# Row means of a 32 x 512 x 1024 array: rows laid out by partition, sums on two engines, and a last tile loaded in shrinking pieces

## The chip, the core and the metric

The kernel runs on one core of a Trainium2 chip. The metric is device time in microseconds (us); a smaller number is better. Three runs of the kernel before gave 173.33, 173.07 and 173.38 us, a median of 173.33.

Names used below: VectorE (DVE in the profile) and ScalarE (ACT) are the two engines that can sum along a row here. SyncE's queue (SP, SPq) issues the transfers between the chip's main memory and the on-chip memory, and 16 DMA engines carry them out. The on-chip memory has 128 partitions; a tile is a piece of it, written as partitions x elements per partition. A landing is the moment at which a transfer's completion is seen.

## The reference

```python
batch, seq, dim = 32, 512, 1024          # x: float32, divisor: 1024.0

def reference(x, divisor):
    return (np.sum(x, axis=-1) / divisor).astype(np.float32)
```

The input is 32 x 512 = 16384 rows of 1024 float32 numbers, 4 KB each, 67.1 MB in all. The output is one number per row, 64 KB. Each input number is read once and added once, so there is nothing to use again.

## The kernel before

The rows are cut into 16 tiles of 1024 rows (`ntiles`, line 25). Within a tile, partition p holds 8 rows that follow each other in memory (`R = 8`), that is 8192 numbers or 32 KB; partition p + 1 holds the next 32 KB. One tile is thus a contiguous block of 4 MB in main memory.

The loop in line 33 does two things per tile: SyncE issues one load of the tile (line 35), and VectorE sums each of the 8 rows (line 36, one instruction with 8 results per partition) into `res`, a tile of 128 x 16 x 8 that stays on the chip. After the loop one instruction on VectorE multiplies all of `res` by 1/divisor (line 37), and one transfer stores it (line 38). Since `res` holds the 8 results of each tile side by side, while in main memory the 8 results of a tile's partition lie apart from those of the next tile, the store writes 128 x 16 runs of 8 numbers, 32 B each.

The order of the work is set by the program's order on each engine and by buffers. The pool `sb` has three buffers for the tile `t`: the loads of the first three tiles are issued at once, and each later load waits in SyncE's queue until VectorE has summed the tile three back. Loads are carried out in the order of their issue, so a load that is issued while another is under way stands behind it. The three operations of the program touch one another only through these waits: reduction on load, load on reduction three back, scaling on all reductions, store on scaling. ScalarE does nothing.

Of the kernel before, what the change touches and what calls it, by code (L numbers as in the profile page):

```python
# [1 line left out]

# [4 lines left out]


@with_exitstack
def kernel(  # L10
    ctx: ExitStack,
    tc: tile.TileContext,
    x: bass.AP,
    divisor: float,
    out: bass.AP,
):
    nc = tc.nc
    xf = x.flatten_outer_dims()
    N, D = xf.shape
    P = nc.NUM_PARTITIONS  # L20
    scale = 1.0 / float(divisor)

    R = 8
    rows_per_tile = P * R
    ntiles = N // rows_per_tile
    assert ntiles * rows_per_tile == N

    xr = x.tensor.reshape((ntiles, P, R, D)).ap()
    out_v = out.tensor.reshape((ntiles, P, R)).ap().rearrange("t p r -> p t r")

    with tc.tile_pool(name="sb", bufs=3) as pool, tc.tile_pool(name="res", bufs=1) as rpool:
        res = rpool.tile([P, ntiles, R], mybir.dt.float32)
        for i in range(ntiles):
            t = pool.tile([P, R, D], mybir.dt.float32)
            nc.sync.dma_start(out=t, in_=xr[i])
            nc.vector.reduce_sum(out=res[:, i, :], in_=t, axis=mybir.AxisListType.X)  # L36
        nc.vector.tensor_scalar_mul(out=res, in0=res, scalar1=scale)  # L37
        nc.sync.dma_start(out=out_v, in_=res)


# [1 line left out]
_INS = ['x', 'divisor']  # L42
_OUTS = [((32, 512), 'float32')]
#: Inputs that are plain numbers.
_NUMBERS = {'divisor': 1024.0}


def kernel(**inputs):
    import numpy as _np
    import concourse.bacc as _bacc  # L50
    import concourse.tile as _tile
    from concourse import mybir as _mybir
    from concourse.bass_utils import run_bass_kernel_spmd as _run

    nc = _bacc.Bacc("TRN2", target_bir_lowering=False, num_devices=1)  # L55
    arrays, args = {}, []
    for name in _INS:
        if name in _NUMBERS:
            args.append(_NUMBERS[name])
            continue  # L60
        a = _np.ascontiguousarray(inputs[name])
        if a.dtype.kind in "iu":
            a = a.astype(_np.int64)
        arrays[f"in_{name}_dram"] = a
        args.append(nc.dram_tensor(f"in_{name}_dram", a.shape, _mybir.dt.from_np(a.dtype), kind="ExternalInput").ap())
    for i, (shape, dtype) in enumerate(_OUTS):
        dt = _mybir.dt.from_np(_np.dtype(dtype))
        args.append(nc.dram_tensor(f"out_{i}_dram", shape, dt, kind="ExternalOutput").ap())
    with _tile.TileContext(nc) as tc:
        kernel(tc, *args)  # L70
    r = _run(nc, [arrays], core_ids=[0])
    got = tuple(r.results[0][f"out_{i}_dram"] for i in range(len(_OUTS)))
    return got[0]
```

## Time and profile before

| | |
|---|---|
| median of three runs | 173.33 us (173.07 to 173.38) |
| span of the profiled execution, first to last instruction (its own time; nothing around it is recorded) | 171.5 us |
| VectorE busy | 139.2 us (81%), 17 instructions |
| one reduction of a tile (line 36) | 8686 ns, 16 times |
| VectorE idle before reductions, all waiting for a load | 28.5 us, of which 13.1 for the first |
| scaling (line 37) | 226 ns |
| loads: 16 of 4096 KB | 20.4 us from issue to landing (median) |
| store: one of 64 KB | 3.0 us from issue to landing |
| main memory traffic | 67.11 MB read, 0.07 MB written, 392 GB/s over the span |

How to read it: the span is the time of one profiled execution on the core; the medians of the runs include what lies around it as well. In the rows of busy digits, the span is cut into 40 slices, and each digit is the busy share of a slice in tenths. A transfer's time from issue to landing includes the time in which it stands behind earlier ones, so the 20.4 us of a load are more than its own share of the DMA engines' time. In the timeline, the bracket behind an instruction is the idle time of its engine before it and what ended that. A row with "x3" stands for three instructions.

### The profile page before, as it was taken

What the parts mean: (1) busy time and instruction counts of PE and PEld (TensorE: products, weight loads), DVE (VectorE), ACT (ScalarE), POOL (GpSimd) and SP (SyncE); (2) the same over time, 40 slices, a digit from 0 to 9 for tenths busy, and PEclk for the clock granted to TensorE, in tenths of its full rate; (3) what the DMA queues carried; (4) which work ended last, traced back from release to release, by engine and by line L of the source; (5) the groups of instructions that cost most, each with busy time, mean ns of one, the idle gap of its engine ahead of it and who ended that gap; (6) DMA issues with size and microseconds to landing.
All of it is one profiled execution on the core that took longest, in us unless ns stands there. A gap on an engine that the chain in (4) does not pass through costs nothing.

```text
span 171.5 us, 92 instructions
## 1 busy us (share of the span) xinstructions
DVE 139.2 (81%) x17; POOL 0.2 (0%) x4
## 2 busy tenths in 40 slices
DVE  0009979797988979797998979797997979797991
POOL 0000000000000000000000000000000000000000
DMA  7999999999898999999999989898999999996002
GB/s 245 405 451 436 420 466 390 466 390 481 382 481 382 474 413 443 428 428 459 397 466 390 474 382 481 374 481 382 481 397 459 428 428 451 405 466 267 0 0 15
DMA packets 4368, 67.18 MB, mean 392 GB/s; under 512 B 2320, under 2 KB 2320, under 8 KB 2320
## 3 DMA queue, kind: packets, MB, share of 16 engines
q1 hardware_dynamic: 4368, 67.18, 91.7%
HBM read 67.11 MB, written 0.07 MB: 392 GB/s over the span
## 4 chain that ended last, share of the span: by engine, by line
DMA 67%; DVE 31%; issue 0%
DMA t<-in_x_dram 67%; DVE res L36 30%; DVE res L37 0%
## 5 line engine op out<-in xcount | busy, mean ns | idle before, releaser
L36 DVE TENSOR_REDUCE res<-t 128x8 f32<-128x8192 f32 x16 | 139.0, 8686 | 28.5 <-DMA t<-in_x_dram 28.5
L37 DVE TENSOR_SCALAR res<-res 128x128 f32<-128x128 f32 x1 | 0.2, 226 | 0.0
L55 POOL MEMSET const-bfloat16-1.0<- 128x1 bf16 x1 | 0.1, 103 | 0.0
L55 POOL MEMSET const-uint8-127<- 128x1 uint8 x1 | 0.1, 103 | 0.0
L55 POOL MEMSET const-float32-1.0<- 128x1 f32 x1 | 0.1, 100 | 0.0
L55 POOL MEMSET const-float32-0.0<- 128x1 f32 x1 | 0.1, 99 | 0.2 <-issue 0.2
## 6 DMA issues: line engine op xcount, KB each, us to landing
t<-in_x_dram SPq DMA_DIRECT2D x16, 4096.0 KB, 20.4
out_dram<-res SPq DMA_DIRECT2D x1, 64.0 KB, 3.0
```

Source lines behind the costliest of these rows:

```text
L36: nc.vector.reduce_sum(out=res[:, i, :], in_=t, axis=mybir.AxisListType.X)
L37: nc.vector.tensor_scalar_mul(out=res, in0=res, scalar1=scale)
L55: nc = _bacc.Bacc("TRN2", target_bir_lowering=False, num_devices=1)
```

## The change

The layout: partition p now owns the 128 rows from 128 p on (`xr` is partition, row, column). Tile by tile, a partition walks through its own 512 KB; one load takes 8 rows, 32 KB, from each of 128 places that lie 512 KB apart. The results of a partition are then 128 numbers that lie together in the output, and the store writes 128 runs of 512 B.

The sums: of the 8 rows of a tile VectorE takes 5 (one instruction) and ScalarE takes 3 (`act_sum`, one instruction per row: a copy into a scratch tile `junk`, whose running sum is the result).

The buffers: the pool for `t` has five buffers.

The end: 15 tiles of 8 rows per partition are followed by loads of 4, 2 and 1 rows, each with its own tile (`tail0` to `tail2`), and the last row comes in three pieces of 512, 256 and 256 columns into `last`. VectorE sums the half row and the last quarter, ScalarE the quarter between, into `part`; a short instruction adds the three, and another scales the result. The scaling of the other 127 results per partition is a separate instruction ahead of the last quarter's sum.

```diff
-    R = 8
-    rows_per_tile = P * R
-    ntiles = N // rows_per_tile
-    xr = x.tensor.reshape((ntiles, P, R, D)).ap()
-    out_v = out.tensor.reshape((ntiles, P, R)).ap().rearrange("t p r -> p t r")
+    J = N // P
+    xr = x.tensor.reshape((P, J, D)).ap()
+    out_v = out.tensor.reshape((P, J)).ap()
...
-        for i in range(ntiles):
-            t = pool.tile([P, R, D], mybir.dt.float32)
-            nc.sync.dma_start(out=t, in_=xr[i])
-            nc.vector.reduce_sum(out=res[:, i, :], in_=t, axis=mybir.AxisListType.X)
-        nc.vector.tensor_scalar_mul(out=res, in0=res, scalar1=scale)
-        nc.sync.dma_start(out=out_v, in_=res)
+    bulk = [8] * 15
+    tail = [4, 2, 1]
+    pool = ctx.enter_context(tc.tile_pool(name="bulk", bufs=5))
...
+    def act_sum(dst, src):
+        n = src.shape[-1]
+        nc.scalar.activation(junk[:, :n], src, COPY, accum_out=dst)
+
+    def sums(t, j, rows, for_act):
+        d = rows - for_act
+        if d:
+            nc.vector.reduce_sum(out=res[:, j : j + d], in_=t[:, :d, :], axis=AX)
+        for r in range(d, rows):
+            act_sum(res[:, j + r : j + r + 1], t[:, r, :])
+
+    j = 0
+    for rows in bulk:
+        t = pool.tile([P, 8, D], F32, name="t")
+        nc.sync.dma_start(out=t[:, :rows, :], in_=xr[:, j : j + rows, :])
+        sums(t, j, rows, rows * 3 // 8)
+        j += rows
+    for k, rows in enumerate(tail):
+        t = one.tile([P, rows, D], F32, name=f"tail{k}")
+        nc.sync.dma_start(out=t, in_=xr[:, j : j + rows, :])
+        sums(t, j, rows, (rows + 1) // 2)
+        j += rows
+    h, q = D // 2, D // 4
+    last = one.tile([P, D], F32, name="last")
+    for a, b in ((0, h), (h, h + q), (h + q, D)):
+        nc.sync.dma_start(out=last[:, a:b], in_=xr[:, j, a:b])
+    nc.vector.reduce_sum(out=part[:, 0:1], in_=last[:, 0:h], axis=AX)
+    act_sum(part[:, 1:2], last[:, h : h + q])
+    nc.vector.tensor_scalar_mul(out=res[:, :j], in0=res[:, :j], scalar1=scale)
+    nc.vector.reduce_sum(out=part[:, 2:3], in_=last[:, h + q : D], axis=AX)
+    nc.vector.reduce_sum(out=part[:, 3:4], in_=part[:, 0:3], axis=AX)
+    nc.vector.tensor_scalar_mul(out=res[:, j : j + 1], in0=part[:, 3:4], scalar1=scale)
+    nc.sync.dma_start(out=out_v, in_=res)
```

How the instructions of VectorE stand before (-) and now (+), for the whole program; `tail_157` and `tail_162` are the tiles of four rows and of two, and an "x15" stands for fifteen alike.

```order
-L36 TENSOR_REDUCE res<-t 128x8 x16
-L37 TENSOR_SCALAR res<-res 128x128
-L69 UNCONDITIONAL_BRANCH
+L111 UNCONDITIONAL_BRANCH
+L53 TENSOR_REDUCE res<-t 128x5 x15
+L53 TENSOR_REDUCE res<-tail_157 128x2
+L53 TENSOR_REDUCE res<-tail_162 128x1
+L74 TENSOR_REDUCE part<-last 128x1
+L76 TENSOR_SCALAR res<-res 128x127
+L77 TENSOR_REDUCE part<-last 128x1
+L78 TENSOR_REDUCE part<-part 128x1
+L79 TENSOR_SCALAR res<-part 128x1
```

Where one reduction of 8 rows and one scaling followed the last load, there are now seven short instructions behind the last bulk tile's, the scaling of most results among them.

The end of SyncE's queue as it is now, with what each transfer waits for (DMAHW0 to DMAHW7 are the eight completion counters that the loads use in turn, DVE and Activation those of VectorE and ScalarE); `tail_166` is the single row.

```order
L60 DMA t<-in_x_dram 128x8192 [waits DMAHW0_49,DVE_49,Activation_49]
L60 DMA t<-in_x_dram 128x8192 [waits DMAHW1_49,DVE_49,Activation_49]
L65 DMA tail_157<-in_x_dram 128x4096
L65 DMA tail_162<-in_x_dram 128x2048
L65 DMA tail_166<-in_x_dram 128x1024
L73 DMA last<-in_x_dram 128x512 [waits DMAHW2_49]
L73 DMA last<-in_x_dram 128x256 [waits DMAHW3_49]
L73 DMA last<-in_x_dram 128x256 [waits DMAHW4_49]
L80 DMA out_dram<-res 128x128 [waits DMAHW5_49,DVE_49,Activation_49]
```

The loads of four, two and one rows wait for nothing, and the three pieces of the last row wait only for the loads that used the same counter eight loads earlier; the bulk loads wait for both summing engines.

More of the change, by code (lines that the diff above doesn't have):

```diff
@@ L21 @@
     scale = 1.0 / float(divisor)
-    R = 8
-    rows_per_tile = P * R
-    ntiles = N // rows_per_tile
-    assert ntiles * rows_per_tile == N
-    xr = x.tensor.reshape((ntiles, P, R, D)).ap()
-    out_v = out.tensor.reshape((ntiles, P, R)).ap().rearrange("t p r -> p t r")
-    with tc.tile_pool(name="sb", bufs=3) as pool, tc.tile_pool(name="res", bufs=1) as rpool:
-        res = rpool.tile([P, ntiles, R], mybir.dt.float32)
-        for i in range(ntiles):
-            t = pool.tile([P, R, D], mybir.dt.float32)
-            nc.sync.dma_start(out=t, in_=xr[i])
-            nc.vector.reduce_sum(out=res[:, i, :], in_=t, axis=mybir.AxisListType.X)
-        nc.vector.tensor_scalar_mul(out=res, in0=res, scalar1=scale)
-        nc.sync.dma_start(out=out_v, in_=res)
+    J = N // P
```

12 lines of the change are left out of this document (added).

## The prediction

> **What bounds the kernel now.** First the page: who is busy, and when. Then the chain of work that ended last, the waits, and the transfers of one tile's period; last the end of the timeline and the store.
>
> ```profile
> span 171.5 us, 92 instructions
> DVE 139.2 (81%) x17; POOL 0.2 (0%) x4
> DVE  0009979797988979797998979797997979797991
> DMA  7999999999898999999999989898999999996002
> L36 DVE TENSOR_REDUCE res<-t 128x8 f32<-128x8192 f32 x16 | 139.0, 8686 | 28.5 <-DMA t<-in_x_dram 28.5
> t<-in_x_dram SPq DMA_DIRECT2D x16, 4096.0 KB, 20.4
> out_dram<-res SPq DMA_DIRECT2D x1, 64.0 KB, 3.0
> ```
>
> VectorE is busy for 81% of the span, but the transfers' row is at 8 or 9 from the second slice to the fifth from the end: two resources run nearly full, and the end of the DMA row (6002) shows them idle while VectorE alone still works. Which of them sets the pace in the middle, the timeline tells: each reduction starts about 9.7 us after the one before, takes 8.69, and waits a little over 1 us for its tile. The last rows are the end of the program.
>
> ```profile
> 13.09 8.69 DVE L36 TENSOR_REDUCE res<-t 128x8 f32<-128x8192 f32 x1 [13.09 <-DMA t<-in_x_dram]
> 22.78 8.69 DVE L36 TENSOR_REDUCE res<-t 128x8 f32<-128x8192 f32 x1 [1.01 <-DMA t<-in_x_dram]
> ...
> 149.06 8.69 DVE L36 TENSOR_REDUCE res<-t 128x8 f32<-128x8192 f32 x1 [1.03 <-DMA t<-in_x_dram]
> 158.76 8.69 DVE L36 TENSOR_REDUCE res<-t 128x8 f32<-128x8192 f32 x1 [1.02 <-DMA t<-in_x_dram]
> 167.48 0.23 DVE L37 TENSOR_SCALAR res<-res 128x128 f32<-128x128 f32 x1
> 167.74 0.40 SPq L38 DMA_DIRECT2D out_dram<-res  x1
> ```
>
> From 13.09 to 158.76 there are 15 periods: 145.67 / 15 = 9.71 us for a tile of 4.19 MB. The next rows are the windows view: first the second half of the first tile's transfer, then exactly one period, then the two microseconds around the store. Its columns are length, VectorE busy, GpSimd busy, clock, share of the 16 DMA engines, GB/s.
>
> ```profile
> 8.00:13.09 5.09, 0.00 (x0) 0.00 (x0) 1.00 0.96 412
> 13.09:22.80 9.71, 8.70 (x2) 0.00 (x0) 1.00 1.00 432
> 168.70:169.70 1.00, 0.00 (x0) 0.00 (x0) 1.00 0.77 53
> 169.70:170.70 1.00, 0.00 (x0) 0.00 (x0) 1.00 0.19 12
> ```
>
> In a period the 16 engines are busy for a share of 1.00 and move 432 GB/s: 4.19 MB / 432 GB/s = 9.71 us. So the loads bound the kernel until 158.74, and the reductions lie under them. From there on nothing is left to load, and what follows is a chain: 8.70 us of reduction of the whole last tile, 0.23 us of scaling, 3.0 us of store, 0.8 us to the end of the span (167.74 + 3.0 = 170.7; 171.5 − 170.7 = 0.8). The span is therefore 13.09 (first tile) + 145.67 + 12.75 (from the last landing on). Only the last term, and 16 x 9.71 = 155.4 us of transfer, are large enough for this change to touch.
>
> **The change, part by part.** The sum is made against the profiled execution's 171.5 us of span; the runs' median of 173.33 stands 1.8 us above it, and I add that again at the end.
>
> Split sums, larger pool, bulk: 15 tiles keep their 4 MB and 8 rows. VectorE now has 5 rows, at 8686/8 = 1086 ns a row 5.4 us, and ScalarE has 3. Both fit beneath 9.71 us, so the split is worth nothing in the bulk: it removes work from an engine that was waiting 1.02 us per tile anyway. ScalarE has no row in this trace; by VectorE's row a sum of 1024 costs 1.09 us, and it would have to take 9.71/3 = 3.2 us before it held back the buffers. Five buffers in place of three: a load now waits for both engines, but for the tile five back. Three already kept the queue fed (share 1.00), so this is worth nothing either; its cover is that a tile is free 5.4 us after landing with four loads still queued.
>
> Seven loads in place of the last one: the four bulk periods before them stay queued. The bytes are the same, so at 432 GB/s the last one lands where the last tile did, 158.74, plus what the extra packets cost. The pieces have 128 rows each as a full tile has, so there are 6 x 128 = 768 more packets, 48 per engine, and 6 more completions. The store shows what tiny packets cost: 2048 rows of 32 B took (0.77 + 0.19) = 0.96 us of each engine, 128 packets each, 7.5 ns a packet. 48 such are 0.36 us; a completion that rides along counts as one more. Bounds: 0 (overlapped) and twice that, 0.7; I take 0.25, since each packet here also has bytes to move. Landing of the last quarter: 159.0.
>
> The Trainium skill speaks against cutting transfers up: "DMA: Bandwidth & Descriptors", Measured, advises at least 1 MiB a transfer, and its fit in the section on the anatomy of one DMA gives each a fixed cost of about 2 us. Six more would by that be an estimated 12 us. The trace disagrees for transfers that queue behind each other: with 20.4 us from issue to landing two tiles are under way at a time, and the period is bytes over 432 GB/s with nothing left for a fixed cost. The small ones queue too: their own tiles need no buffer back, and the waits that the last three have on earlier loads' completion counters are for tiles 10 to 12 (counted from 0), which land by 129.6.
>
> The tail of sums, which replaces 8.70 + 0.23. At 432 GB/s (1.21 us for a row piece of 0.52 MB) the pieces land at 159.0 (last quarter), 158.7, 158.4 (half row), 157.8 (one row), 156.6 (two) and 154.1 (four), and the 15th bulk tile at 149.1. VectorE: 5 rows to 154.5, two rows to 156.7, one row to 157.8. So it is free when the half row lands at 158.4. 512 elements at 1.06 ns (8686/8192) are 0.54; the scaling row (226 ns for 128 elements) shows that a small instruction has a fixed part, so 0.54 to 0.77: I take 0.65, to 159.05. Scaling 127 sums: 0.23, to 159.3; it waits for ScalarE's sum of the single row, landed 157.8, with 1.09 done at 158.9, in time by 0.15. Quarter: 0.27 to 0.50, take 0.40, to 159.7. Adding three partial sums and scaling one number: each 0.05 to 0.23 by the scaling row, take 0.15, to 160.0; with hand-offs of about 0.03 (the last reduction ends at 167.45, its scaling starts at 167.48), 160.1. ScalarE's quarter lies beside this (158.9 + 0.4). So the store is issued at 160.1 in place of 167.74: −7.6 us.
>
> The store: 128 rows of 512 B in place of 2048 of 32 B. At 432 GB/s its 64 KB need 0.15 us of the engines, not 0.96: −0.8, and no less than 0 nor more than −0.96. So 3.0 becomes 2.2.
>
> Sum: 171.5 − 7.6 − 0.8 = 163.1 of span, and with 1.8 around it **164.9 us**. The unknowns of this sum, all at their good ends, give 164.0 (DVE steps −0.55, packets −0.25, store −0.15), and at their bad ends 166.5 (steps +0.3, packets +0.45, store +0.8).
>
> The layout is the part with no row. Now one partition's data for all tiles lie together, so the 128 rows of one load are 512 KB apart in memory (128 x 4 KB), where before they followed each other at 32 KB. Each packet still reads one run of 32 KB. If only the DMA engines set the pace, 432 GB/s stays. What speaks for that: the period is the same to 0.02 us in all 15 tiles, as an engine's fixed rate would make it. The lowest rate of a full queue that the trace shows is 412 GB/s, in the first tile (4.6% below); the highest is 432. I take 432, and the 412 for the range: 4.6% of 155.4 us is 7.2 us.
>
> The Trainium skill has a rule on this: "DMA: Bandwidth & Descriptors", Latency and other measured facts, says that copies of 128-partition tiles from main memory to main memory lose rate at large power-of-two row pitches, 207 GB/s per direction at 512 KiB against 214 with a padded pitch, and far less from 2 MiB on. By that ratio the estimate is 3.3% of the transfer time, about 5 us, and a total near 170. No run here shows a pitch of 512 KiB.
>
> **The rivals.**
>
> *The row pitch costs rate, up to 5.4%.* Mechanism: the 16 engines read at addresses a large power of two apart and meet in the same part of memory, so a packet takes longer. For: all 16 engines are at a share of 1.00, so any delay shows in full. Against: before, they also read at powers of two apart, and the rate was flat. Each per cent costs 1.55 us; at 412 GB/s the time is 164.9 + 7.2 = 172.1, at half of that 168.5. This is the skill's rule above. Chance 0.18.
>
> *The same, more than 5.4%: slower.* The gain of 8.4 us is gone when 155.4 us become 163.8, a period of 10.24 us, 410 GB/s. At 400 GB/s the period is 10.48 and the time 177. The point lies just under the slowest stretch of before, 412. Chance 0.06.
>
> *The small transfers show their fixed cost.* The first tile took 12.34 us from issue to landing, 9.71 of them bytes, in this row of the chain of waits:
>
> ```profile
> 0.73 12.34 DMA t<-in_x_dram
> ```
>
> So 2.6 us is the price of one that nothing hides. Were it paid for all six extra ones, 15.8 us: 180.7. It decides from 1.4 us each. Against stands the period without a gap. Chance 0.02 for slower, and 0.04 for a part of it, or for a ScalarE that takes over 1.6 us a row and so comes last at the end: 166.5 to 172.
>
> *The split does nothing.* True in the bulk, as shown; the gain is all in the tail. If the tail's pieces did nothing either, the reduction of 8.7 us would still be gone from the end, since at most one quarter row is left: a result within 0.2% needs a loss elsewhere that happens to match. Chance 0.02.
>
> **How the numbers follow.** The forecast, 164.9 with its own range of 164.0 to 166.5, has the remaining 0.68. The range for 8 in 10 reaches over the first rival to a rate loss of 3% (164.9 + 4.7): 164.0 to 169.5; this holds nearly all of the 0.68, two thirds of the 0.18 and most of the 0.04. About 0.2% is what a measurement of this kernel can tell from no change (the runs span 173.07 to 173.38). Faster: 0.68 + 0.18 + 0.04 = 0.90. Same: 0.02. Slower: 0.06 + 0.02 = 0.08.
>
> **What would show it.** In the profile after: bulk reductions of 5 rows starting every 9.71 us, near 5.4 us each, with waits of some 4.3 us for the load (pitch harmless); a period of 10 or more is the first rival. The last load landing at 159.0: later with the period unchanged means that small pieces cost. The store issued at 160.1, landing 2.2 later; and VectorE, not ScalarE, as the last to feed it. The prediction is wrong if the period moves by over 0.1 us, or if more than 2 us lie between the last landing and the store.

## The result, and the profile after

The changed kernel takes 164.85 us (median of four runs, 164.67 to 165.25) against 173.23 us (173.07 to 173.38): a ratio of 0.952, 95% interval 0.9506 to 0.9537. The forecast was 164.9. As the experiments show, some of its terms were off and cancelled each other.

The page of the changed kernel, its lines of busy time, the digits in 40 slices, and its groups:

```profile
span 162.9 us, 222 instructions
DVE 87.1 (53%) x22; ACT 58.1 (36%) x101; POOL 0.2 (0%) x4
DVE  0007639094571917549093672908448092763983
DMA  6999999999999999999999999999999999999990
...
L53 DVE TENSOR_REDUCE res<-t 128x5 f32<-128x5120 f32 x15 | 82.3, 5488 | 72.5 <-DMA t<-in_x_dram 72.5
L48 ACT ACTIVATE junk<-t 128x1024 f32<-128x1024 f32 x45 | 46.2, 1027 | 99.2 <-DMA t<-in_x_dram 98.3
L48 ACT ACTIVATION_READ_ACCUMULATOR junk<-t 128x1 f32 x45 | 8.4, 186 | 0.0
...
out_dram<-res SPq DMA_DIRECT2D x1, 64.0 KB, 1.5
```

The DMA row, which ended in 6002, now stays at 9 up to and including the last slice but one. VectorE went from 81% of the span to 53%, and that by itself bought nothing: its idle time before the bulk sums grew from 28.5 to 72.5 us. A sum on ScalarE is two instructions, 1027 ns and a readout of 186 ns.

The timeline of the changed kernel, VectorE's and SyncE's rows from the last bulk tiles on:

```profile
139.65 5.49 DVE L53 TENSOR_REDUCE res<-t 128x5 f32<-128x5120 f32 x1 [4.22 <-DMA t<-in_x_dram]
...
149.36 5.49 DVE L53 TENSOR_REDUCE res<-t 128x5 f32<-128x5120 f32 x1 [4.22 <-DMA t<-in_x_dram]
...
154.76 3.40 DVE L53 TENSOR_REDUCE res<-tail 128x2 f32<-128x2048 f32 x2
...
158.75 0.69 DVE L74 TENSOR_REDUCE part<-last 128x1 f32<-128x512 f32 x1 [0.59 <-DMA last<-in_x_dram]
...
159.36 0.22 DVE L76 TENSOR_SCALAR res<-res 128x127 f32<-128x127 f32 x1
159.49 0.41 DVE L77 TENSOR_REDUCE part<-last 128x1 f32<-128x256 f32 x1
...
160.00 0.15 DVE L78 TENSOR_REDUCE part<-part 128x1 f32<-128x3 f32 x1
160.19 0.15 DVE L79 TENSOR_SCALAR res<-part 128x1 f32<-128x1 f32 x1
160.41 0.35 SPq L80 DMA_DIRECT2D out_dram<-res  x1
```

The period is 149.36 − 139.65 = 9.71 us as before. From the half row's landing on, VectorE works almost without a break (the longest gap is 0.1 us): the last quarter, issued at 129.9 and landed 29.4 us later, at 159.3, is there 0.2 us before its sum starts, so it is not its landing that sets the end but VectorE's five short instructions. The store is issued 7.33 us earlier than before, lands after 1.5 us instead of 3.0, and 1.0 us follows instead of 0.8: 7.3 + 1.5 − 0.2 = 8.6 = 171.5 − 162.9.

Where the store's 1.5 us went, two windows views show, first of before, then of the changed kernel (for the changed kernel a column of ScalarE's busy time is added after VectorE's):

```profile
168.60:168.80 0.20, 0.00 (x0) 0.00 (x0) 1.00 0.21 12
168.80:169.00 0.20, 0.00 (x0) 0.00 (x0) 1.00 1.00 63
169.00:169.20 0.20, 0.00 (x0) 0.00 (x0) 1.00 0.75 55
...
169.80:170.00 0.20, 0.00 (x0) 0.00 (x0) 1.00 0.55 34
```

```profile
161.00:161.20 0.20, 0.00 (x0) 0.00 (x0) 0.00 (x0) 1.00 0.00 0
161.20:161.40 0.20, 0.00 (x0) 0.00 (x0) 0.00 (x0) 1.00 0.56 169
161.40:161.60 0.20, 0.00 (x0) 0.00 (x0) 0.00 (x0) 1.00 0.57 159
161.60:161.80 0.20, 0.00 (x0) 0.00 (x0) 0.00 (x0) 1.00 0.00 0
```

In the trace the 2048 runs of 32 B last from 168.72 to 169.98, 1.26 us from the first packet to the last; the 128 runs of 512 B take 0.35. The prediction had priced the packets at the engines' mean busy time, 0.96, but the landing comes after the last packet, and the busy share was mostly near 0.75 in between. The other 0.5 us lie ahead of and behind the packets: 0.98 us from the issue to the first packet became 0.84, and 0.75 from the last packet to the landing became 0.35. Why these two stretches shrank was not tested.

### The profile page after: what moved, and what is told of

Its sections match the earlier page's. It is cut to its first block, busy times and chain, and to the rows that moved or that the text cites. A ratio compares the mean times of both kernels' runs of the same rounds, so it can differ in the third digit from the quotient of the medians.

```text
span 162.9 us, 222 instructions
## 1 busy us (share of the span) xinstructions
DVE 87.1 (53%) x22; ACT 58.1 (36%) x101; POOL 0.2 (0%) x4
## 3 DMA queue, kind: packets, MB, share of 16 engines
q1 hardware_dynamic: 3168, 67.18, 96.5%
## 4 chain that ended last, share of the span: by engine, by line
DMA 90%; DVE 7%; issue 1%; SPq 0%; DVEq 0%
DMA t<-in_x_dram 61%; DMA last<-in_x_dram 30%; DVE res L53 7%; DVE part L77 0%; DVE res L76 0%; DVE part L78 0%; DVE res L79 0%; SPq L60 0%; DVE part L74 0%; DVEq L78 0%
## 5 line engine op out<-in xcount | busy, mean ns | idle before, releaser
L53 DVE TENSOR_REDUCE res<-t 128x5 f32<-128x5120 f32 x15 | 82.3, 5488 | 72.5 <-DMA t<-in_x_dram 72.5
L48 ACT ACTIVATE junk<-t 128x1024 f32<-128x1024 f32 x45 | 46.2, 1027 | 99.2 <-DMA t<-in_x_dram 98.3
L48 ACT ACTIVATION_READ_ACCUMULATOR junk<-t 128x1 f32 x45 | 8.4, 186 | 0.0
L48 ACT ACTIVATE junk<-tail 128x1024 f32<-128x1024 f32 x4 | 4.1, 1028 | 1.7 <-DMA tail<-in_x_dram 1.7
L53 DVE TENSOR_REDUCE res<-tail 128x2 f32<-128x2048 f32 (+1 forms) x2 | 3.4, 1743 | 0.0
L74 DVE TENSOR_REDUCE part<-last 128x1 f32<-128x512 f32 x1 | 0.7, 685 | 0.6 <-DMA last<-in_x_dram 0.6
L48 ACT ACTIVATION_READ_ACCUMULATOR junk<-tail 128x1 f32 x4 | 0.7, 186 | 0.0
```

What stands on the lines that cost most here:

```text
L48: nc.scalar.activation(junk[:, :n], src, COPY, accum_out=dst)
L53: nc.vector.reduce_sum(out=res[:, j : j + d], in_=t[:, :d, :], axis=AX)
L74: nc.vector.reduce_sum(out=part[:, 0:1], in_=last[:, 0:h], axis=AX)
```

## The experiments

Every kernel was compared with the kernel before, run on the same chip. The changed kernel itself was run once more near the end (e12), since its own time differs between groups of runs by more than some of the effects.

**e1: the layout alone, in the kernel before.**

```diff
-    xr = x.tensor.reshape((ntiles, P, R, D)).ap()
-    out_v = out.tensor.reshape((ntiles, P, R)).ap().rearrange("t p r -> p t r")
+    xr = x.tensor.reshape((P, ntiles, R, D)).ap()
+    out_v = out.tensor.reshape((P, ntiles, R)).ap()
...
-            nc.sync.dma_start(out=t, in_=xr[i])
+            nc.sync.dma_start(out=t, in_=xr[:, i])
```

> The kernel before with the new layout alone (and so the store of 512 B rows): 16 loads of 4 MB, rows of one load 512 KB apart, all sums on VectorE. Theory (the pitch costs nothing, the store gains 1.5 us as in the profile after, where 3.0 us became 1.5): period 9.71 us, 173.2 - 1.5 = 171.7 us. Rival (the pitch costs rate and something else in the changed kernel made up for it): a period above 9.75, and at the 3.3% of the prediction's first rival 10.03 and 176.8 us.

Measured: 172.71 us (172.17 to 172.85), ratio 0.9965 (0.9952 to 0.9979). That is neither theory's time: 0.5 us faster than before, where 1.5 was expected. The timeline of e1:

```profile
13.38 8.69 DVE L36 TENSOR_REDUCE res<-t 128x8 f32<-128x8192 f32 x1 [13.38 <-DMA t<-in_x_dram]
23.09 8.69 DVE L36 TENSOR_REDUCE res<-t 128x8 f32<-128x8192 f32 x1 [1.02 <-DMA t<-in_x_dram]
...
159.07 8.69 DVE L36 TENSOR_REDUCE res<-t 128x8 f32<-128x8192 f32 x1 [1.02 <-DMA t<-in_x_dram]
167.79 0.23 DVE L37 TENSOR_SCALAR res<-res 128x128 f32<-128x128 f32 x1
168.04 0.35 SPq L38 DMA_DIRECT2D out_dram<-res  x1
```

The period is 9.71 us throughout, so the rate is not lost as the rival has it, and the store lands in 1.6 us. But the first tile comes 0.29 us later than before, and this profiled run has the shortest span of the five (170.4; the others 170.6 to 171.1). The store's gain is there and part of it is given back by something that varies from run to run. e9 to e12 go after that.

**e2: pieces, but every sum on VectorE.**

```diff
-        sums(t, j, rows, rows * 3 // 8)
+        sums(t, j, rows, 0)
...
-        sums(t, j, rows, (rows + 1) // 2)
+        sums(t, j, rows, 0)
...
-    act_sum(part[:, 1:2], last[:, h : h + q])
+    nc.vector.reduce_sum(out=part[:, 1:2], in_=last[:, h : h + q], axis=AX)
```

> The changed kernel with every sum on VectorE, pieces kept. Theory (the split is worth its time only behind the last bulk tile, where VectorE falls behind the loads): VectorE is done with the last bulk tile at 149.36 + 8.69 = 158.05, then 4.42 + 2.28 + 1.21 + 0.69 + 0.41 + 0.2 + 0.41 + 0.4 us in a row, store issued near 168.0 in place of 160.4: 172.4 us, nearly all of the gain gone. Rival (the pieces alone bring the gain, since the sums lie under the loads): within 2 us of 164.9.

Measured: 172.3 us (171.76 to 172.82), ratio 0.9949 (0.9929 to 0.9969). The theory holds: without a second engine the pieces are worth almost nothing. VectorE's end in the timeline of e2:

```profile
150.44 8.69 DVE L53 TENSOR_REDUCE res<-t 128x8 f32<-128x8192 f32 x1 [1.03 <-DMA t<-in_x_dram]
159.04 7.73 DVE L53 TENSOR_REDUCE res<-tail 128x4 f32<-128x4096 f32 x3
166.69 0.68 DVE L74 TENSOR_REDUCE part<-last 128x1 f32<-128x512 f32 x1
```

After 150.44 there is no wait left: the pieces lie on the chip long before VectorE comes to them.

**e3 and e4: the split in the pieces only; in the last bulk tile and the pieces.**

```diff
-        sums(t, j, rows, rows * 3 // 8)
+        sums(t, j, rows, 0)                                # e3
+        sums(t, j, rows, rows * 3 // 8 if j == 112 else 0) # e4
```

> The changed kernel with VectorE taking all 8 rows of each of the 15 bulk tiles; the pieces at the end stay split. Theory (backlog): VectorE leaves the last bulk tile at 158.05, not 154.8, then 2.28 + 1.21 + 0.69 + 0.15 + 0.41 + 0.4: store near 163.2, 167.7 us. Rival (the prediction's step as written: the split is worth nothing in the bulk): 164.9 us.

> The changed kernel with the split in the last of the 15 bulk tiles and in the pieces only; VectorE sums all 8 rows of the first 14. Theory (only the last bulk tile's backlog matters): 164.9 us, within 0.3. Rival (the split in the bulk helps in another way, by freeing buffers earlier): slower by over 0.5 us.

Measured: e3 167.41 us (167.2 to 167.98), ratio 0.9672 (0.9655 to 0.9689); e4 165.0 us (164.6 to 165.42), ratio 0.952 (0.9506 to 0.9534), the changed kernel's own ratio in the first runs. So the split is worth 2.4 us in the 15th bulk tile and nothing that these runs show in the 14 before it. The timeline of e3 at that place, then of e4:

```profile
150.13 8.69 DVE L53 TENSOR_REDUCE res<-t 128x8 f32<-128x8192 f32 x1 [1.02 <-DMA t<-in_x_dram]
158.74 3.40 DVE L53 TENSOR_REDUCE res<-tail 128x2 f32<-128x2048 f32 x2
162.06 0.68 DVE L74 TENSOR_REDUCE part<-last 128x1 f32<-128x512 f32 x1
```

```profile
150.18 5.49 DVE L53 TENSOR_REDUCE res<-t 128x5 f32<-128x5120 f32 x1 [1.03 <-DMA t<-in_x_dram]
155.58 3.40 DVE L53 TENSOR_REDUCE res<-tail 128x2 f32<-128x2048 f32 x2
159.48 0.69 DVE L74 TENSOR_REDUCE part<-last 128x1 f32<-128x512 f32 x1 [0.50 <-DMA last<-in_x_dram]
```

In e4 VectorE waits 0.50 us for the half row: it has caught up. In e3 it is 2.6 us behind by then.

**e5: the split without the pieces.**

```diff
-    bulk = [8] * 15
-    tail = [4, 2, 1]
+    bulk = [8] * 16
```

The loads and sums of `tail` and `last` are gone; one instruction scales all of `res`.

> The changed kernel without the pieces: 16 loads of 8 rows, each summed 5 to 3, one scaling of all results, one store. Theory (the pieces cost the loads little and shorten the last sums): the last tile lands near 159.0, VectorE takes 5.49 us, scaling 0.23, store near 164.8 in place of 160.4: 169.2 us. Rival (the small loads cost a good part of what they bring): the last tile lands 1 us or more before the changed kernel's last quarter, and the time is under 168 us.

Measured: 169.96 us (169.77 to 170.38), ratio 0.9815 (0.9802 to 0.9828). The mechanism is as the theory has it: 5.49 us of sum behind the last landing. The rival falls, since the last tile did not land early. It landed late; the timeline of e5:

```profile
13.35 5.49 DVE L51 TENSOR_REDUCE res<-t 128x5 f32<-128x5120 f32 x1 [13.35 <-DMA t<-in_x_dram]
23.97 5.49 DVE L51 TENSOR_REDUCE res<-t 128x5 f32<-128x5120 f32 x1 [5.13 <-DMA t<-in_x_dram]
33.69 5.49 DVE L51 TENSOR_REDUCE res<-t 128x5 f32<-128x5120 f32 x1 [4.23 <-DMA t<-in_x_dram]
...
159.94 5.49 DVE L51 TENSOR_REDUCE res<-t 128x5 f32<-128x5120 f32 x1 [4.20 <-DMA t<-in_x_dram]
```

The second tile came 10.62 us after the first, 0.9 more than a period, and all later ones kept that delay. That accounts for the missing part of the expectation (169.2 against 169.96).

**e6 and e7: 120 loads of one row per partition in place of the 15 bulk loads; 512 KB apart, and next to each other.**

```diff
-    for rows in bulk:
-        t = pool.tile([P, 8, D], F32, name="t")
-        nc.sync.dma_start(out=t[:, :rows, :], in_=xr[:, j : j + rows, :])
-        sums(t, j, rows, rows * 3 // 8)
-        j += rows
+    for n in range(sum(bulk)):
+        t = pool.tile([P, 1, D], F32, name="t")             # bufs=40
+        nc.sync.dma_start(out=t, in_=xr[:, j : j + 1, :])   # e7: xc[:, j : j + 1, :]
+        sums(t, j, 1, 1 if n % 8 in (2, 4, 7) else 0)
+        j += 1
```

In e7 `xc` is `x.tensor.reshape((J, P, D)).ap().rearrange("j p d -> p j d")`.

> The changed kernel with its 15 bulk loads of 8 rows cut into 120 loads of one row per partition (0.52 MB, runs of 4 KB, 512 KB apart); VectorE sums 5 of every 8 rows, ScalarE 3, room for 40 rows. Theory (a queued transfer costs only its packets, 7.5 ns each as the store of before showed): 840 more packets per engine, 6.3 us: 171.2 us. Rival (a fixed cost per transfer that queueing does not hide): at only 0.5 us each, 105 more loads are 52 us, over 215 us.

> As the kernel with row loads, but each of the 120 loads reads 128 rows that follow each other in memory, 4 KB apart; the pieces at the end stay as they are. It sums other rows into the places of the output (the first 15360 rows in another order, the rest partly again), the same amount of work. Theory (the distance between a load's rows does not matter to the rate): the same as the row loads 512 KB apart within 0.5 us, 171.2. Rival (the pitch costs where runs are short): this one faster by 3% or more, some 5 us.

Measured: e6 173.86 us (172.78 to 174.64), ratio 1.0031 (1.001 to 1.0053); e7 173.14 us (172.68 to 174.47), ratio 1.0006 (0.9987 to 1.0025). Nothing like a fixed cost of 0.5 us or more per transfer appears, but the 171.2 of both theories was too low as well, by 2.7 and 1.9 us. A stretch of the windows view of e6:

```profile
33.00:53.00 20.00, 11.72 (x11) 6.89 (x12) 0.00 (x0) 1.00 1.03 410
```

410 GB/s in place of 432: with 16 engines a packet of 4 KB takes 160 ns, where at 432 GB/s it would take 152, so 8 ns more. Since e6 has both more packets and more loads, the rate alone does not say which of the two costs. The packets in the changed kernel's trace do: the median one of 4 KB takes 160 ns, of 16 KB 611 and of 32 KB 1213, that is 37.6 ns per KB and 8 to 10 ns whatever the size. 840 more packets and 105 more completions per engine at 8 ns are 7.6 us; 173.86 lies 8.2 us above the changed kernel on that chip (165.71, e12), 0.08 us for each of the 105 more loads. The expectation had 6.3, having counted 7.5 ns and left out the completions, and started from 164.9. e7 ran at 409 to 411 GB/s too: rows 512 KB apart do not lower the rate of the stream even with runs of 4 KB. The 0.7 us between the two are more than the 0.5 of e7's theory, but the intervals overlap, and the rival's 3% is not there.

**e8: three buffers.** The edit is `bufs=3` for the pool `bulk`.

> The changed kernel with three buffers for the bulk tiles in place of five. Theory (three keep the load queue full, since a tile is free 5.5 us after it lands and two more are queued): 164.9 us, within 0.3. Rival (five are needed, because a load now waits for two engines): a period above 9.75 us, over 165.5.

Measured: 165.26 us (164.84 to 165.79), ratio 0.9543 (0.9524 to 0.9561); its interval overlaps both of the changed kernel's (0.9506 to 0.9537 in the first runs, 0.9555 to 0.9581 in e12). The period is 9.71 in its profile, but for one tile 0.35 and one 0.21 us late. Five buffers were not needed for a full queue; whether they are worth some tenths of a microsecond does not show.

**e9 to e12: how far apart the rows of one load lie.** All have the split, the pieces and five buffers; `B` is the number of blocks of the input, and the rows of a load are 512 KB / B apart.

```diff
-    xr = x.tensor.reshape((P, J, D)).ap()
-    out_v = out.tensor.reshape((P, J)).ap()
+    L = J // B                                   # B = 16 (e9), 4 (e10), 2 (e11)
+    xb = x.tensor.reshape((B, P, L, D)).ap()
+    out_v = out.tensor.reshape((B, P, L)).ap().rearrange("b p l -> p b l")   # e9: as in the changed kernel
...
-        nc.sync.dma_start(out=t[:, :rows, :], in_=xr[:, j : j + rows, :])
+        nc.sync.dma_start(out=t[:, :rows, :], in_=xb[j // L][:, j % L : j % L + rows, :])
```

> The changed kernel with the rows of one load next to each other as before (32 KB apart, 16 blocks); the results are still stored in 512 B rows, and so land in another order. Theory (the distance of 512 KB costs something after all, where the loads start: the first tile landed at 13.38 in place of 13.09, and in most profiles of the new layout one or two of the first five tiles came 0.2 to 0.9 us late): first tile at 13.1, no late tile, 0.3 to 1.0 us below the changed kernel beside it, with less spread between runs. Rival (the delays come from something else, the split or the queue): the same as the changed kernel beside it within 0.2 us.

> The changed kernel with the input in four blocks: a load's rows 128 KB apart, stored as 512 runs of 128 B, results in their right places. Theory (delay only at 512 KB): the loads as with near rows, the store dearer by 0.1 to 0.4 us: 0.1 to 0.8 us below the changed kernel beside it. Rival (no delay from the distance): slower than it by the store's 0.1 to 0.4 us.

> As with four blocks, with two: rows 256 KB apart, 256 runs of 256 B. Theory (the delay grows with the distance): between the four blocks and the changed kernel in its late tiles. Rival: the same as the changed kernel, plus 0.1 us of store.

> The changed kernel again, beside the three others on the same chip: 164.9 us, first tile near 13.4; a late tile among the first five in this profile or not, and runs spread over 0.5 us or more, if the delays are the layout's.

| | rows apart | runs of the store | median (lowest to highest), us | ratio (interval) |
|---|---|---|---|---|
| e9 | 32 KB | 512 B, another order | 164.44 (164.34 to 164.66) | 0.9502 (0.9489 to 0.9515) |
| e10 | 128 KB | 128 B | 164.75 (164.67 to 164.98) | 0.9518 (0.9505 to 0.9531) |
| e11 | 256 KB | 256 B | 164.73 (164.70 to 164.97) | 0.9518 (0.9505 to 0.9531) |
| e12, the changed kernel | 512 KB | 512 B | 165.71 (165.29 to 165.86) | 0.9568 (0.9555 to 0.9581) |

The theory holds against its rival: the distance of 512 KB costs 1.3 us in these runs (e12 against e9, which stores the same runs), more than the 0.3 to 1.0 expected, though not by the rate of the stream. The size varies: against the changed kernel's first runs, 164.85, e9 is 0.4 us faster and the intervals overlap. Halving the distance removes most of the cost (e11's interval lies below e12's), and the store with 256 runs lands in 1.7 us, with 512 runs in 1.8, against 1.6 in e12. That the delay grows with the distance, as e11's expectation had it, does not show. VectorE's first rows in the timeline of e12, then of e9:

```profile
13.33 5.49 DVE L53 TENSOR_REDUCE res<-t 128x5 f32<-128x5120 f32 x1 [13.33 <-DMA t<-in_x_dram]
23.65 5.49 DVE L53 TENSOR_REDUCE res<-t 128x5 f32<-128x5120 f32 x1 [4.84 <-DMA t<-in_x_dram]
...
62.63 5.49 DVE L53 TENSOR_REDUCE res<-t 128x5 f32<-128x5120 f32 x1 [4.34 <-DMA t<-in_x_dram]
72.78 5.49 DVE L53 TENSOR_REDUCE res<-t 128x5 f32<-128x5120 f32 x1 [4.66 <-DMA t<-in_x_dram]
```

```profile
13.01 5.49 DVE L55 TENSOR_REDUCE res<-t 128x5 f32<-128x5120 f32 x1 [13.01 <-DMA t<-in_x_dram]
22.70 5.49 DVE L55 TENSOR_REDUCE res<-t 128x5 f32<-128x5120 f32 x1 [4.20 <-DMA t<-in_x_dram]
...
71.27 5.49 DVE L55 TENSOR_REDUCE res<-t 128x5 f32<-128x5120 f32 x1 [4.23 <-DMA t<-in_x_dram]
```

With a full queue the wait is 4.22 us; a larger one is a late tile. e12 has late tiles of 0.62, 0.12 and 0.44 us and a first tile 0.32 us later than e9's; e9 has none in that stretch. In the trace's packets, e12's late tiles are moments at which eight packets at once take up to 2.3 us in place of 1.21. Such moments are there in the profiles of e2, e3, e4, e5 and e8 as well, all with 512 KB, but not in e1's nor in the changed kernel's first profile, which therefore was a good one. Of the eight profiles with 32 KB packets and 512 KB, six have them after the first 5 us; of the four with less (before, e9, e10, e11) none has. The first tile is summed from 13.29 to 13.38 us on in all eight, and from 12.73 to 13.09 on in the four.

Around 100 us e10 and e11 also have one late tile, 0.4 and 0.5 us; e9 has 0.1 there. The tile in the timeline of e10, and the queues' packets of e10 between 93.5 and 96.5 us:

```profile
100.55 5.49 DVE L55 TENSOR_REDUCE res<-t 128x5 f32<-128x5120 f32 x1 [4.66 <-DMA t<-in_x_dram]
```

```profile
q1 hardware_dynamic: 34, 1.11, 87.3%
q14 instruction: 1, 0.01, 0.7%
```

On another queue (q14), marked "instruction", one packet of 8 KB runs for 0.32 us from 94.52 us on, and the load packet that starts as it ends takes 1.59 us in place of 1.21. So this late tile is of another kind: one packet, not eight. The profiles of e5, e8, e9, e12 and the changed kernel have such a pair too, with a tile at most 0.1 us late; what decides that was not tested.

## Why the prediction was right, and where it was not

*The bound.* Right: the loads set the pace before and after, 9.71 us a tile and 432 GB/s, and all that was to be had lay behind the last landing.

*The bulk.* "The split is worth nothing in the bulk" was wrong for one tile. The step's own reason, that VectorE waits there anyway, holds for 14 tiles (e4), but the 15th one's sum is what VectorE carries into the pieces: 2.4 us (e3 against e4). The sum itself was not hurt, because it took the 5 rows of that tile into the count of the tail. The rival "The split does nothing" had the same fault: it held that the reduction of 8.7 us would be gone from the end in any case, and e2 shows that without the split the store is issued no earlier than before (168.56 against 167.74). e2 and e5 show how little each half brings alone, all with the new layout: pieces without the split 172.3, the split without pieces 169.96, both together 165.

*More, smaller loads.* Right in size: the last quarter landed 9.97 us after the 15th bulk tile (149.34 and 159.31), where a full tile of before took 9.70, so the extra packets cost 0.27 us and 0.25 was forecast. The count behind it was off: six loads, not seven, replace the last one, so there are five more transfers and 640 more packets (40 per engine), which at 7.5 ns takes 0.06 us off the estimate; and the rival that charges 2.6 us for each extra one comes to 13, not 15.8. The prediction's argument that the period leaves nothing for a fixed cost could not show it, since 432 GB/s is that period's own bytes over its time; e6 shows it: queued transfers cost 8 ns per packet. The page "DMA: Bandwidth & Descriptors" of the Trainium skill gives its fixed cost of 2 us per transfer (the section on the anatomy of one DMA) for transfers that GpSimd issues. SyncE's queue here, kept full, does not show it: 0.08 us for each more load in e6. The page's advice of 1 MiB or more is right here in direction, since e6 with 0.5 MB is 8 us slower, but for the number of packets.

*The tail of sums.* Right nearly to the instruction: 0.69, 0.22, 0.41, 0.15 and 0.15 us against 0.65, 0.23, 0.40, 0.15 and 0.15. ScalarE takes 1.18 us from row to row with the readout, not 1.09, and its last quarter was still done (159.81) before VectorE had its own (159.90). Its sum of the single row, which the scaling waits for, was done at 159.27, in time by 0.09 and not by 0.15; in e11 and e12 it is the last to release the scaling, without a visible cost (0.60 us from the half row's sum to the scaling, 0.61 in the first profile). The store was issued 7.33 us earlier, not 7.6, and the 0.3 between them are the first tile's delay.

*The store.* The term was mis-sized: −1.5 measured, −0.8 forecast, and the bound of −0.96 was no bound. It came from the mean busy time of the engines, where the time from the first packet to the last and the stretches before and after the packets count.

*The row pitch.* The mechanism that the first rival named was put in the wrong place. The stream's rate did not fall (9.71 us a tile in e1, and in e12 between its late tiles), so the 412 GB/s of the bound was not seen. That bound was no slower rate to begin with: in the kernel before, 140 to 149 us gives 411 GB/s and 140 to 149.71, a whole period, 432, so where a window's edges fall makes that difference alone. Nor was the 207 to 214 GB/s of the Trainium skill's page ("DMA: Bandwidth & Descriptors", Latency and other measured facts), which is for copies within main memory and would have been some 5 us, seen for loads at 512 KB. But the forecast was wrong to put the distance at nothing: there is a later first tile, and there are single moments at which packets stall, in all 0.3 us in the changed kernel's first profile (the first tile alone) and 1.3 us in the runs of e12. That forecast and measurement agree to 0.05 us is luck. In the profile 0.7 us more from the store stood against that 0.3 and against 0.2 us more at the very end, so the span was 0.2 us below the forecast (162.9 against 163.1), and the median of the runs lies 0.2 above the profiled one (164.85 against 164.67). In the runs of e12 the same sum would have been 0.8 us too low.

*Open.* That 512 KB costs time is shown by e9 to e12, and that the moments with eight slow packets go with it by the profiles, one for each run; what makes eight packets stall at once is not. How many pieces the end needs, and how small, was not tested either. The best version tried that gives the results in their places is e10 or e11: about 1 us below the changed kernel beside them, but only 0.1 below its first runs, which is not clear.

## What to carry to other kernels

Look for the time behind the last landing: when loads bound a kernel at a rate that cannot be raised, that is where most of what can be shortened lies. Shrinking pieces help only if the engines have no backlog when the pieces arrive, so here the split had to begin one tile earlier. Price a store by its number of runs, and by the whole time from issue to landing, not by bytes or by the engines' mean busy time. When a layout is chosen for the sake of the store, a middle one (two or four blocks) can keep most of the store's gain and spare the loads a distance that cost up to 1.3 us here.

## What was not expected of the hardware

A packet of a queued load costs 8 ns besides its bytes, so 32 KB packets run at 432 GB/s and 4 KB ones at 410. A sum on ScalarE shows as two instructions, the second a readout of 186 ns. And with the rows of one load 512 KB apart, the stream keeps its 9.71 us a tile, but the first tile comes about 0.3 us later, and later ones by up to 0.9 us (e5) at single moments when eight packets at once take 1.5 to 2.6 us in place of 1.21. Such moments were not seen at 32, 128 or 256 KB; the one late tile there, by 0.1 to 0.5 us, came with a single slow packet beside an 8 KB packet of the instruction queue.
